# Down stage of a hybrid diffusion layer: earlier modulation rows, earlier first-half outputs, a longer last batch and another order of closing the tiles

## Chip, cores and metric

The kernel runs on one core of a Trainium2 chip. The metric is the device time of one execution in microseconds (us); lower is better. TensorE (PE) does the matmuls, VectorE (DVE), ScalarE (ACT) and GpSimd (POOL) the elementwise work, and SyncE (SP) issues most DMAs. Each engine works through its own queue in order, and semaphores order the engines among each other.

## What is computed

One layer of a diffusion backbone on 512 sample tokens and 128 prompt tokens with 1024 features: gated token mixers, then a feed-forward part with a short convolution. Only the last matrix product and what follows it are touched by the change:

```python
sh1, sc1, g1, sh2, sc2, g2 = jnp.split(mod, 6, axis=-1)   # mod = silu(c) @ w_ada + b_ada
...
h = rmsnorm(x, lw['norm2_g']) * (1.0 + sc2) + sh2
x = x + g2 * conv_ffn(h, ...)          # ends in (silu(g) * a) @ w_down, w_down is 2816 x 1024
...
y = rmsnorm(x, final_norm_g)           # x * rsqrt(mean(x*x) + EPS) * final_norm_g
```

So each output row needs both column halves of the down product before its mean square is known, and only then can it be scaled and stored.

## The kernel before

**Precision.** Each f32 operand is split into a high part (ScalarE, a copy that rounds to the matmul's type) and a low part (VectorE, the difference). A product is three matmuls: high with high, high with low, low with high.

**Blocks.** The 512 sample tokens are two blocks of 256, that is token tiles 0 and 1, and tiles 2 and 3; the 128 prompt tokens are tile 4. The 2816 inner features are two groups of 11 steps of 128 (called k steps), the 1024 output columns are two halves of 512. The sample part is a product of 2x2 blocks done in seven block products instead of eight (Winograd's form of Strassen's method). The prompt tile rides along in four of them.

**Units.** `PHASES` lists the seven products in the order 1, 5, 6, 2, 7, 4, 3; each is cut into six units of two k steps (the sixth has one), so there are 42 units, numbered u = 0 to 41 (`DOWN[u]` is phase and place j in it). A unit has a load (`down_load`), a preparation (`down_prep`: the splits, L1855 to L1859, after a sum of operands in `x_sum`) and its matmuls (`down_tile`, L1960). When unit i's matmuls are written, the load of unit i+5 and the preparation of unit i+3 have just been written (`ahead`). Five slots are cycled: a preparation overwrites what unit u-5 used. The fifth slot's weights lie in region X0 up to u = 28 and in A behind that.

**Units that are held back.** A unit in `JOIN` is kept and its matmuls are run together with the next ones, tile by tile, so that a tile is closed earlier than the others. Before, units (6,3) and (6,4) are held, and the last batch is (6,3), (6,4), (6,5): five k steps for tile 0, then five for tile 1, then for the prompt tile 4, which is cut into two column parts of 256 (`halved`), each with a PSUM bank of its own. What the prompt tile has gathered up to (6,2) is corrected and added to x by three VectorE instructions (L1967, then L1977 and L1981).

**What follows a product** is written in `down_start` and `down_out`. `LATER` names the phase and unit at which an output is written: `out_11(t)` forms the first column half of tiles 0, 1 and 4, `out_22(t)` the second half of tiles 2 and 3. Each is `joined`: a sum or difference with a kept product, the multiplication with the modulation row g2 (`gained`, L1977), the addition to the residual x (`added`, L1981), and a square with a row sum on ScalarE (`half_one`, L1986). The remaining halves come straight from the last products through `half_two`: `gained`, `added`, square with sum (L2045), joining both halves' sums (`half_join`, L2062), the root as a power of -0.5 on POOL (`down_root`, L2065), then scaling the one half on ScalarE (`down_scale`, L2073) and the other on VectorE (`down_gain`, L2080), and the store. `down_scale` expects its half to be multiplied with the final norm's gain already: that is `final_gain` on POOL (L2007).

**Modulation rows.** The last columns of w_ada (numbers 45, 46 and 47, which belong to g2) are made by VectorE in `col_make`: each is two multiplications with row sum over 128x1024 (L285). They are loaded by `col_load`. `gain_rows(1)` transposes the result on TensorE (L304), ScalarE copies it, SP writes it to DRAM (L308), and `gain_load` broadcasts it into S0 (L312). `COLS` and `G2` give the units at which this is done.

**Order.** The framework's scheduler may issue an instruction earlier than it is written, if it is ready. `tc.keep_in_program_order` (`keep_`) pins an instruction behind everything that was written before it for the same engine. `x2r` loads the residual tiles: 0 and 1 into X0, 2 and 3 into X1, 4 into G; these DMAs are pinned on SP.

Of the kernel before, what the change touches and what calls it, by code (L numbers as in the profile page):

```python
# [16 lines left out]
P = 128  # L17
# [53 lines left out]
def tile_step(ctx: ExitStack, tc: tile.TileContext, a: dict, outs: list, dbg=None):  # L71
# [54 lines left out]
    def nm(s):  # L126
        cnt[0] += 1
        return f"{s}_{cnt[0]}"

    def region(tag, shape, dt=F32):  # L130
        return big.tile(shape, dt, tag=tag, name=nm(tag))

    def pm():
        return psm.tile([P, 512], F32, tag="m", name=nm("m"))
# [165 lines left out]

    def gain_rows(i):

        m = pm() if i == 0 else acc["p"]
        ten.transpose(m[0:16, 0:P], gcol[:, i].rearrange("p v f -> p (v f)"), ident)  # L304
        pe(0.11)
        g = sp.tile([16, P], F32, tag="gr", name=nm("gr"), bufs=1)
        act(g, m[0:16, 0:P], AF.Copy)
        nc.sync.dma_start(growd[i], g)  # L308
# [1457 lines left out]
    def x2r(tag):  # L1766
        if tag not in x2v:
            r = x2v[tag] = region(tag, [P, 1280 if tag == "G" else 2560])
            for i in range(1 if tag == "G" else 2):
                sync(r[:, i * D:(i + 1) * D], x2d[i + dict(X0=0, X1=2, G=4)[tag]])  # L1770
        return x2v[tag]
# [36 lines left out]
    PHASES = [(1, "w", 0, (0, 0), 0), (5, "s", 0, (0, 1), 0), (6, "s", 1, (0, 0), None), (2, "w", 1, (1, 0), 1),  # L1808
              (7, "s", 2, (0, 1), None), (4, "s", 3, (1, 1), None), (3, "w", 3, (1, 0), 1)]
    DOWN = [(ph, j) for ph in range(7) for j in range(6)]  # L1810
    JOIN = {(4, 4), (5, 0), (6, 3), (6, 4)}

    def down_load(u):
        ph, j = DOWN[u]
# [24 lines left out]
    def down_prep(u, raw):  # L1839
        ph, j = DOWN[u]  # L1840
        ks, (p_, _, _, (h, c), hp) = KS[j], PHASES[ph]
        n = len(ks)
        if u % 5 < 3:
            w = wp.tile([P, 2, 2, 512], F32R, tag="w", name=nm("w"))
        elif u % 5 == 3:
            if "w4" not in fx:
                fx["w4"] = region("MG1", [P, 2, 2, 512], F32R)
            w = fx["w4"]
        else:
            w = region("X0" if u < 29 else "A", [P, 2, 2, 512], F32R)  # L1850
        if "xs" not in fx:
            fx["xs"] = region("XH", [P, 5, 2, 2, 256], F32R), region("MG0", [P, 5, 2, 2, P], F32R)
        s = [x[:, u % 5] for x in fx["xs"]]
        x_sum(p_, ks)
        act(w[:, 0, 0:n], raw, AF.Copy)  # L1855
        for x, r in zip(s, [x_raw(h, c, ks)] + ([xr["p", hp][:, ks[0]:ks[-1] + 1]] if hp is not None else [])):
            act(x[:, 0, 0:n], r, AF.Copy)
            vec.tensor_tensor(x[:, 1, 0:n], r, x[:, 0, 0:n].bitcast(F32), ALU.subtract)  # L1858
        vec.tensor_tensor(w[:, 1, 0:n], raw, w[:, 0, 0:n].bitcast(F32), ALU.subtract)  # L1859
        return w, s  # L1860
# [38 lines left out]
            pass  # L1899
        gain_col(f, ar[0])  # L1900

    COLS = dict(zip((23, 21, 19), range(47, 44, -1)))
    G2 = 27

    def down_start(u):
        ph, j = DOWN[u]
        if u == 0:
            acc["b1"], acc["b2"] = [pm(), pm()], [pm(), pm()]
            g0, g1 = pg(), pg()
            acc["p"], acc["q"], acc["b3"] = g0[:, 0, :], g0[:, 1, :], [g1[:, 0, :], g1[:, 1, :]]  # L1910
            r = region("XL1", [P, 5, 512])
            acc["c1"], acc["u2"], acc["cp"] = [r[:, 0], r[:, 1]], [r[:, 2], r[:, 3]], r[:, 4]
        for tag, part in {0: (("A", 0), ("B", 0)), 2: (("A", 1), ("B", 1)), 9: (("D", 0),), 11: (("D", 1),),
                          13: (("F", None),)}.get(u, ()):
            x_load(tag, part)
        if u == 5:
            x_tail(1, 1)
        if u == 16:
            x2[2:4] = [x2r("X1")[:, 0:1024], x2r("X1")[:, 1024:2048]]
        if u + 2 in COLS and COLS[u + 2] > 45:  # L1920
            col_load(COLS[u + 2])
        if u in COLS:
            col_make(COLS[u])
        if u == G2 - 1:
            gain_rows(1)
        if u == G2:
            grows["g2"] = gain_load(1, "S0")
            x2[4] = x2r("G")[:, 0:1024]
            r = region("H", [P, 2, 512])
            acc["u3"] = [r[:, 0], r[:, 1]]  # L1930
        if u == 28:
            x2[0:2] = [x2r("X0")[:, 0:1024], x2r("X0")[:, 1024:2048]]
        for f in LATER.get((ph, j), ()):
            f()

# [5 lines left out]
    def down_tile(u, ws):  # L1941
        ph, j = DOWN[u]
        p_, _, _, _, hp = PHASES[ph]
        down_start(u)
        hold.append((KS[j], ws))
        if (ph, j) in JOIN:
            return
        batch = hold[:]
        hold.clear()
        end = j == 5  # L1950
        for t in (0, 1, 4) if hp is not None else (0, 1):
            halved = p_ == 3 and t == 4 and end
            for ci, (c0, c1) in enumerate(((0, 256), (256, 512)) if halved else ((0, 512),)):
                ps = (acc["b1"][ci] if halved else bank(p_, t))[:, 0:c1 - c0]
                o = 0 if t == 4 else t * P
                for bi, (ks, (w, s)) in enumerate(batch):
                    for k in range(len(ks)):
                        for i, (hx, hw) in enumerate(((0, 0), (0, 1), (1, 0))):
                            first = ks[k] == 0 and i == 0 and (p_ in (1, 5) or p_ == 2 and t < 4) or halved and bi == k == i == 0
                            mm(ps, s[t // 4][:, hx, k, o:o + P], w[:, hw, k, c0:c1], start=first,  # L1960
                               stop=i == 2 and bi == len(batch) - 1 and k == len(ks) - 1, skip_group_check=True)
                        tick(0.65 * (c1 - c0) / 512)
                if end:
                    down_out(p_, t, c0, c1, ps)
        if p_ == 3 and j == 2:
            y = gp.tile([P, 512], F32, tag="gt", name=nm("y"))
            vec.tensor_tensor(y, acc["q"], acc["cp"], ALU.subtract)  # L1967
            gained(1, 4, 0, 512, y)
            added(1, 4, 0, 512)
# [19 lines left out]
    def down_out(p_, t, c0, c1, ps):  # L1989
        if p_ == 2 and t == 4:  # L1990
            act(acc["yp"], ps, AF.Copy)
        elif p_ in (1, 6):
            act(acc["cp"] if t == 4 else acc["c1" if p_ == 1 else "u2"][t], ps, AF.Copy)
        elif p_ == 7:
            act(acc["u3"][t], ps, AF.Copy)
        elif p_ == 4:
            half_two(0, t + 2, 0, 512, ps)
        elif p_ == 3:
            if t < 4:
                y = gp.tile([P, 512], F32, tag="gt", name=nm("y"))  # L2000
                keep_(vec.tensor_tensor(y, ps, acc["u2"][t], ALU.subtract))  # L2001
                ps = y
            half_two(1, t, c0, c1, ps)

    def final_gain(nh, t):
        xs = x2[t][:, nh * 512:nh * 512 + 512]
        pool.tensor_tensor(xs, xs, xr["F"][:, nh * 512:nh * 512 + 512], ALU.mult)  # L2007

    def final_gains():
        for nh, t in ((1, 2), (1, 3), (0, 0), (0, 1), (0, 4)):  # L2010
            final_gain(nh, t)
            if t in (2, 3):
                down_store(0, t)

    def joined(nh, t, ps, x, op):
        y = gp.tile([P, 512], F32, tag="gt", name=nm("y"))
        vec.tensor_tensor(y, ps, x, op)  # L2017
        gained(nh, t, 0, 512, y)
        added(nh, t, 0, 512)
        half_one(nh, t)  # L2020

    def out_11(t):
        if t == 4:
# [6 lines left out]
    def out_22(t):  # L2030
        joined(1, t + 2, acc["b2"][t], acc["u3"][t], ALU.subtract)

    LATER = {(5, 1): (lambda: out_22(0),), (5, 3): (lambda: out_22(1),), (5, 5): (lambda: out_11(0),),
             (6, 1): (lambda: out_11(1),), (6, 2): (lambda: out_11(4),), (6, 3): (final_gains,)}

    def half_two(nh, t, c0, c1, ps):
        xs = x2[t][:, nh * 512 + c0:nh * 512 + c1]
        q1, q2 = (st3[:, i + t:i + t + 1] for i in (8, 16))
        keep_(gained(nh, t, c0, c1, ps))
        if t == 4 and c0 == 0:  # L2040
            half_join(1, 8)
            down_root(1)
        keep_(added(nh, t, c0, c1))
        if c0 == 0:
            keep_(act(prods[t], xs, AF.Square, accum_out=q1))  # L2045
        if t == 1:
            down_store(nh, 0)
        elif t < 4:
            half_join(t, 8)
            down_root(t)  # L2050
        elif c0 > 0:
            half_join(t, 8)
            down_scale(nh, 1)
            keep_(vec.scalar_tensor_tensor(prods[t], xs, 1.0, xs, ALU.mult, ALU.mult, accum_out=q2))
            half_join(t, 16)
            down_root(t)
            down_gain(nh, 1)
            down_store(nh, t)

    def half_join(t, i):  # L2060
        q = st3[:, t:t + 1]
# [366 lines left out]
```

## Time and profile before

| what | us |
|---|---|
| median of three runs | 1009.75 (1008.81 to 1010.03) |
| profiled execution, its own time | 1008.12 |
| its span in the trace | 1006.0 |
| first matmul of the down stage | 858.4 |
| last matmul's end | 997.6 |

The span runs from the first to the last instruction. In a timeline a line gives the start, the length, the engine, the kernel's line, the operation and how many instructions were merged; matmuls are pipelined, so the spacing of their starts, not their length, is what one costs. TensorE's granted clock is full (1.00) in every stretch of the down stage up to 997.6.

### The profile page before, as it was taken

To read this page: it belongs to the slowest core of one execution; us is meant where nothing else is said; L and a number is where in the kernel's file an instruction comes from. 1 tells how busy PE (TensorE), PEld (TensorE's weight loads), DVE (VectorE), ACT (ScalarE), POOL (GpSimd) and SP (SyncE) were. 2 spreads that over 40 slices of the span, in tenths; PEclk is the share of its full clock that TensorE was granted. 3 is DMA by queue.
4 is the path that set the end of the run, shared out by engine and by line. 5 is a ranking of instruction groups with operands and counts; after the bars stand their busy time and mean duration, and the time that the engine had idled before them with its cause. 6 is when DMAs were issued, how large, how long until landed. Compare 5 with 4: busy or idle time off the path is not lost. (4 is left out here: it accounts for less than half of the span.)

```text
span 1006.0 us, 18962 instructions
## 1 busy us (share of the span) xinstructions
PE 993.2 (99%) x7503; PEld 941.0 (94%) x7503; DVE 825.0 (82%) x1381; ACT 558.5 (56%) x983; POOL 168.4 (17%) x223
## 2 busy tenths in 40 slices
PE   8999999999999999999999999999999999999996
PEld 7899999999999999999998899999999999888885
DVE  6678899867765767767768878999999998988897
ACT  6642343445554444445445476777777777656563
POOL 1000020323210221331010021222222222100023
PEclk9999999999999999999999999999999999999998
DMA  9875344496495498898258683866666666886462
GB/s 354 332 251 165 108 149 126 126 262 211 106 296 186 173 244 189 262 296 180 81 201 324 272 315 118 253 153 173 177 166 166 176 171 193 320 298 229 156 245 105
DMA packets 70009, 208.93 MB, mean 208 GB/s; under 512 B 9632, under 2 KB 24768, under 8 KB 67232
## 3 DMA queue, kind: packets, MB, share of 16 engines
q1 hardware_dynamic: 43536, 148.60, 41.8%
q0 software_dynamic: 26384, 59.12, 25.4%
q8 instruction: 59, 0.97, 0.4%
q14 instruction: 30, 0.25, 0.1%
HBM read 165.99 MB, written 48.51 MB: 213 GB/s over the span
## 5 line engine op out<-in xcount | busy, mean ns | idle before, releaser
L375 PE MATMUL g<-XH,w 128*128 128x320 f32 x704 | 171.2, 317 | 0.1
L375 PEld LDWEIGHTS g<-XH,w 128*128 128x128 f32 x704 | 120.6, 188 | 2.7 <-issue 1.0
L375 PE MATMUL g<-XL,w 128*128 128x320 f32 x352 | 108.7, 309 | 0.0
L375 PEld LDWEIGHTS g<-XL,w 128*128 128x128 f32 x352 | 66.3, 188 | 0.0
L1960 PE MATMUL m<-w,XH 128*128 128x512 f32 x246 | 58.6, 390 | 0.0
L1960 PEld LDWEIGHTS m<-w,XH 128*128 128x128 f32 x246 | 46.1, 188 | 9.7
L1152 PE MATMUL m<-XH,w 128*128 128x320 f32 x224 | 52.5, 309 | 0.0
L151 POOL DMA_DIRECT2D wsum<-in_w_dn_dram x36 | 36.5, 1158 | 53.1 <-issue 41.8
L151 DVE SCALAR_TENSOR_TENSOR X<-MG,p2t,X 128x641 f32<-128x641 f32 x44 | 38.9, 884 | 1.0 <-ACT X L151 0.2
L151 DVE SCALAR_TENSOR_TENSOR X<-X,p2t,X 128x641 f32<-128x641 f32 x44 | 38.9, 883 | 0.9
L151 ACT ACTIVATE w<-raw 128x1024 fp32r<-128x1024 f32 (+3 forms) x46 | 38.2, 851 | 2.1 <-DMA raw<-in_w_in_dram 1.1
L1512 PE MATMUL g<-XL,w 128*128 128x320 f32 x240 | 38.6, 310 | 0.0
L1152 PEld LDWEIGHTS m<-XH,w 128*128 128x128 f32 x224 | 38.3, 188 | 0.0
L1512 PE MATMUL g<-XL,C 128*128 128x320 f32 x240 | 38.3, 309 | 0.0
L1512 PEld LDWEIGHTS g<-XL,w 128*128 128x128 f32 x240 | 36.0, 188 | 0.6 <-ACT MG L151 0.3
L1512 PEld LDWEIGHTS g<-XL,C 128*128 128x128 f32 x240 | 36.0, 188 | 0.0
L1152 PE MATMUL m<-XL,w 128*128 128x320 f32 x112 | 34.6, 309 | 0.0
L151 ACT ACTIVATE ga<-m,cst 128x320 f32<-128x320 f32 x27 | 14.2, 528 | 36.6 <-PE m L1152 36.6
L1859 DVE TENSOR_TENSOR w<-raw,w 128x1024 fp32r<-128x1024 f32 (+1 forms) x26 | 30.1, 1159 | 3.3 <-ACT w L1855 3.3
L151 DVE TENSOR_TENSOR w<-raw,w 128x1024 fp32r<-128x1024 f32 (+2 forms) x36 | 30.6, 871 | 1.2 <-ACT w L151 1.2
L151 DVE TENSOR_TENSOR gb<-g,gb 128x640 f32<-128x640 f32 x12 | 9.9, 825 | 26.3 <-PE g L1165 25.4
L336 ACT ACTIVATE w<-raw 128x1024 fp32r<-128x1024 f32 (+1 forms) x22 | 24.3, 1104 | 12.2 <-PE m L947 8.2
(582 smaller groups left out, 2920.0 us busy)
## 6 DMA issues: line engine op xcount, KB each, us to landing
wsum<-in_w_dn_dram POOLq DMA_DIRECT2D x30, 512.0 KB, 12.1
raw<-in_w_up_dram SPq DMA_DIRECT2D x30, 512.0 KB, 5.3
raw<-in_w_gp_dram SPq DMA_DIRECT2D x21, 640.0 KB, 6.5
raw<-in_w_in_dram SPq DMA_DIRECT2D x19, 512.0 KB, 4.4
H<-in_w_adt_dram SPq DMA_DIRECT2D x19, 512.0 KB, 4.1
raw<-wsum SPq DMA_DIRECT2D x12, 512.0 KB, 4.4
actx<-X POOLq DMA_DIRECT2D x22, 256.0 KB, 5.0
wsum<-wsum POOLq DMA_DIRECT2D x10, 512.0 KB, 11.0
```

The source lines that it names most:

```text
L151: r = f(*args, **kw)
L336: high = lambda: act(w[:, 0], raw, AF.Copy)
L375: mm(o, w[:, h, k0 + k, :], r(k)[:, s], start=(k == 0 and i == 0), stop=(k == kt - 1 and i == 2))
L1152: mm(o, w[:, k, :], x[:, k, :], start=(first and k == 0 and j == 0), stop=(k == 3 and j == 2), skip_group_check=True)
L1512: z = mm(o, w[:, k, :], x[:, k, :], start=(first and k == 0 and j == 0), stop=(k == 3 and j == 2), skip_group_check=True)
L1859: vec.tensor_tensor(w[:, 1, 0:n], raw, w[:, 0, 0:n].bitcast(F32), ALU.subtract)
L1960: mm(ps, s[t // 4][:, hx, k, o:o + P], w[:, hw, k, c0:c1], start=first, stop=i == 2 and bi == len(batch) - 1 and k == len(ks) - 1, skip_gr ...
```

## The change

The last three modulation columns are made at units 9, 11 and 13 instead of 19, 21 and 23, and g2 is loaded at unit 16 instead of 27. The transposition uses another PSUM bank. The fifth weight slot lies in X1 (but for unit 4), so that X0 can take the residual of tiles 0 and 1 at unit 18, and X1 that of tiles 2 and 3 at unit 27. The first-half outputs `out_11(0)`, `out_11(1)`, `out_11(4)` are written at the first three units of the fifth phase (4,0) to (4,2) instead of (5,5), (6,1) and (6,2). The subtraction of a kept product from the last product's tiles 0 and 1 is taken out of the end: a new `out_less` multiplies the kept product with g2 and subtracts it from x at (4,3) and (4,4). The last batch has seven k steps ((6,2) is held too), and the prompt tile is cut into 320 and 192 columns. POOL's five final gains are pinned, written at (6,2) and (6,3), and the stores of tiles 2 and 3 behind the first two. In `half_two`, tile 0 is finished and stored at once, and tile 1 is joined, rooted, scaled and stored as soon as the first part of the prompt tile is added.

```diff
-        m = pm() if i == 0 else acc["p"]
+        m = pm() if i == 0 else acc["b3"][0]
...
-    JOIN = {(4, 4), (5, 0), (6, 3), (6, 4)}
+    JOIN = {(4, 4), (5, 0), (6, 2), (6, 3), (6, 4)}
...
-            w = region("X0" if u < 29 else "A", [P, 2, 2, 512], F32R)
+            w = region("X0" if u == 4 else "X1" if u < 29 else "A", [P, 2, 2, 512], F32R)
...
-    COLS = dict(zip((23, 21, 19), range(47, 44, -1)))
-    G2 = 27
+    COLS = dict(zip((13, 11, 9), range(47, 44, -1)))
+    G2 = 16
...
-        if u == 16:
-            x2[2:4] = [x2r("X1")[:, 0:1024], x2r("X1")[:, 1024:2048]]
+        if u == 18:
+            x2[0:2] = [x2r("X0")[:, 0:1024], x2r("X0")[:, 1024:2048]]
...
-        if u == 28:
-            x2[0:2] = [x2r("X0")[:, 0:1024], x2r("X0")[:, 1024:2048]]
+        if u == 27:
+            x2[2:4] = [x2r("X1")[:, 0:1024], x2r("X1")[:, 1024:2048]]
...
-            for ci, (c0, c1) in enumerate(((0, 256), (256, 512)) if halved else ((0, 512),)):
+            for ci, (c0, c1) in enumerate(((0, 320), (320, 512)) if halved else ((0, 512),)):
...
-        if p_ == 3 and j == 2:
+        if p_ == 3 and j == 1:
...
-            if t < 4:
-                y = gp.tile([P, 512], F32, tag="gt", name=nm("y"))
-                keep_(vec.tensor_tensor(y, ps, acc["u2"][t], ALU.subtract))
-                ps = y
             half_two(1, t, c0, c1, ps)
...
-        pool.tensor_tensor(xs, xs, xr["F"][:, nh * 512:nh * 512 + 512], ALU.mult)
-
-    def final_gains():
-        for nh, t in ((1, 2), (1, 3), (0, 0), (0, 1), (0, 4)):
+        keep_(pool.tensor_tensor(xs, xs, xr["F"][:, nh * 512:nh * 512 + 512], ALU.mult))
+
+    def final_gains(*which):
+        for nh, t in which:
             final_gain(nh, t)
-            if t in (2, 3):
-                down_store(0, t)
+
+    def stores():
+        for t in (2, 3):
+            down_store(0, t)
...
+    def out_less(t):
+        gained(1, t, 0, 512, acc["u2"][t])
+        xs = x2[t][:, 512:1024]
+        vec.tensor_tensor(xs, xs, prods[t], ALU.subtract)
...
-    LATER = {(5, 1): (lambda: out_22(0),), (5, 3): (lambda: out_22(1),), (5, 5): (lambda: out_11(0),),
-             (6, 1): (lambda: out_11(1),), (6, 2): (lambda: out_11(4),), (6, 3): (final_gains,)}
+    LATER = {(4, 0): (lambda: out_11(0),), (4, 1): (lambda: out_11(1),), (4, 2): (lambda: out_11(4),),
+             (4, 3): (lambda: out_less(0),), (4, 4): (lambda: out_less(1),), (5, 1): (lambda: out_22(0),), (5, 3): (lambda: out_22(1),),
+             (6, 2): (lambda: final_gains((1, 2), (1, 3)), stores),
+             (6, 3): (lambda: final_gains((0, 0), (0, 1), (0, 4)),)}
...
         keep_(gained(nh, t, c0, c1, ps))
+        keep_(added(nh, t, c0, c1))
+        if c0 == 0:
+            keep_(act(prods[t], xs, AF.Square, accum_out=q1))
         if t == 4 and c0 == 0:
             half_join(1, 8)
             down_root(1)
-        keep_(added(nh, t, c0, c1))
-        if c0 == 0:
-            keep_(act(prods[t], xs, AF.Square, accum_out=q1))
-        if t == 1:
-            down_store(nh, 0)
-        elif t < 4:
+            down_store(nh, 1)
+        elif t != 1:
             half_join(t, 8)
+            if t == 4:
+                keep_(vec.scalar_tensor_tensor(prods[t], xs, 1.0, xs, ALU.mult, ALU.mult, accum_out=q2))
+                half_join(t, 16)
             down_root(t)
-        elif c0 > 0:
-            half_join(t, 8)
-            down_scale(nh, 1)
-            keep_(vec.scalar_tensor_tensor(prods[t], xs, 1.0, xs, ALU.mult, ALU.mult, accum_out=q2))
-            half_join(t, 16)
-            down_root(t)
-            down_gain(nh, 1)
-            down_store(nh, t)
+            if t != 2 and t != 3:
+                down_store(nh, t)
```

## The prediction

> **What bounds the kernel now.** I read the page's busy shares and slices first, then a table of stretches of the down stage.
>
> ```profile
> span 1006.0 us, 18962 instructions
> PE 993.2 (99%) x7503; PEld 941.0 (94%) x7503; DVE 825.0 (82%) x1381; ACT 558.5 (56%) x983; POOL 168.4 (17%) x223
> ...
> 884.60:907.10 22.50, 22.50 (x101) 18.62 (x100) 18.39 (x30) 12.68 (x22) 0.00 (x0) 1.00 0.82 280
> 907.10:922.00 14.90, 14.90 (x67) 12.35 (x66) 12.99 (x18) 9.24 (x15) 0.00 (x0) 1.00 0.73 247
> ...
> 944.50:959.60 15.10, 15.10 (x69) 12.38 (x68) 10.94 (x14) 8.80 (x15) 0.00 (x0) 1.00 0.50 186
> 959.60:974.80 15.20, 15.20 (x67) 12.29 (x66) 15.17 (x21) 10.94 (x20) 5.03 (x3) 1.00 0.71 255
> ...
> 997.60:1006.00 8.40, 0.02 (x1) 0.00 (x0) 4.24 (x12) 3.18 (x7) 1.72 (x2) 0.66 0.48 187
> ```
>
> Columns are the stretch, its length, then PE, PEld, DVE, ACT and POOL busy, the clock, DMA share and GB/s. PE is busy in all of each stretch to 997.6; then comes a tail of 8.4 us without matmuls. The change leaves the number of products as it is, so it can win only in that tail or where PE's starts are spaced wider than a matmul needs. DVE has 4.16 us idle in the fifth phase (944.5 to 959.6) and none in the sixth (15.17 of 15.20). The timeline of PE shows what that costs, and what a matmul needs:
>
> ```profile
> 846.12 1.92 PE L1512 MATMUL g<-XH,w 128*128 128x320 f32 x12
> 847.88 1.92 PE L1512 MATMUL m<-XH,w 128*128 128x320 f32 x12
> ...
> 970.46 3.17 PE L1960 MATMUL m<-A,XH 128*128 128x512 f32 x12
> 973.47 4.24 PE L1960 MATMUL m<-w,XH 128*128 128x512 f32 x18
> ...
> 982.99 2.88 PE L1960 MATMUL m<-MG,XH 128*128 128x512 f32 x12
> ...
> 993.87 0.88 PE L1960 MATMUL m<-A,MG 128*128 128x256 f32 x6
> 994.58 1.24 PE L1960 MATMUL m<-w,MG 128*128 128x256 f32 x9
> 995.66 0.88 PE L1960 MATMUL m<-A,MG 128*128 128x256 f32 x6
> 996.38 1.24 PE L1960 MATMUL m<-w,MG 128*128 128x256 f32 x9
> ```
>
> From 982.99 (the start of unit (6,2)) to 993.87 there are 48 matmuls of 512 columns (18 of that unit, 15 each for tiles 0 and 1): 10.88/48 = 0.2267 us each. Unit 34 at 970.46 takes 3.01 us where 12 x 0.2267 = 2.72: 0.29 us of stall. This is the only stall of that size, so all stalls together are worth some tenths.
>
> **The tail, step by step.** The timeline of the end:
>
> ```profile
> 995.44 0.68 DVE L2001 TENSOR_TENSOR y<-m,XL 128x512 f32<-128x512 f32 x1
> ...
> 997.50 0.74 DVE L2080 SCALAR_TENSOR_TENSOR X<-X,st,F 128x512 f32<-128x512 f32 x1
> ...
> 998.16 0.42 DVE L1977 TENSOR_TENSOR dt<-m,S 128x256 f32<-128x256 f32 x1
> ...
> 998.72 0.72 POOL L2065 TENSOR_TENSOR st<-st,neghalf 128x1 f32<-128x1 f32 x1 [2.57 <-DVE st L2062]
> 998.95 0.42 DVE L1977 TENSOR_TENSOR dt<-m,S 128x256 f32<-128x256 f32 x1
> ...
> 999.40 0.42 DVE L1981 TENSOR_TENSOR G<-G,dt 128x256 f32<-128x256 f32 x1
> ...
> 999.75 0.15 DVE L2062 SCALAR_TENSOR_TENSOR st<-st 128x1 f32<-128x1 f32 x1
> 999.86 0.42 DVE L2054 SCALAR_TENSOR_TENSOR dt<-G 128x256 f32<-128x256 f32 x1
> ...
> 1000.33 0.16 DVE L2062 SCALAR_TENSOR_TENSOR st<-st 128x1 f32<-128x1 f32 x1
> ...
> 1000.57 0.99 POOL L2065 TENSOR_TENSOR st<-st,neghalf 128x1 f32<-128x1 f32 x1 [1.12 <-DVE st L2062]
> 1001.59 0.72 ACT L2073 ACTIVATE G<-G,st 128x512 f32<-128x512 f32 x1 [1.40 <-POOL st L2065]
> ...
> 1002.41 0.33 SPq L1761 DMA_DIRECT2D out_dram<-G  x1
> ```
>
> PE's last matmul (996.38 + 1.24) ends at 997.62, but VectorE takes up the prompt tile's last part only at 998.95, 1.33 us later: it is still closing tile 1 (from 995.44). From 998.95 on nothing else is in the way, and it takes 7.04 us to the end at 1005.99 (3.58 of it behind the store's issue). That queue is what the change attacks.
>
> **PE's end after the change.** The last batch has 21 matmuls for tile 0 and 21 for tile 1, 42 x 0.2267 = 9.52 us, then 21 of 320 columns at (847.88 - 846.12)/12 = 0.1467, 3.08 us, then 21 of 192. That width isn't in the trace. The 256-column ones cost (995.66 - 993.87)/15 = 0.119; the nearest narrower ones are 128 columns wide:
>
> ```profile
> 572.07 1.03 PE L1339 MATMUL m<-cst,C 128*128 128x128 f32 x8
> 572.86 0.95 PE L1295 MATMUL m<-w,B 128*128 128x512 f32 x3
> ```
>
> 8 in 0.79 us, 0.099. Half the width saves only 0.02, so I take 0.11 for 192: 2.31 us (2.08 to 2.50). Sum 14.91 us against 10.88 + 30 x 0.119 = 14.45 before: PE ends **0.46 us later** (0.23 to 0.65). The Trainium skill, "TensorE: Matmul & The Clock Gate", section "LDWEIGHTS (loading the stationary operand)", gives a weight load as columns / 1.2 ns: 107 ns for 128 columns, whatever the matmul's width. An estimate from that page is 2.24 us for the 21, and PE's end 0.39 us later; the row of 0.099 lies below that figure.
>
> **VectorE's chain in the new tail.** Tile 1 needs no subtraction now (0.68 us, L2001, gone), and nothing of it is left when the prompt tile comes. The 320 part's last matmul starts and drains by 982.99 + 9.52 + 3.08 + 0.16 = 995.75 (0.16 is 1.92 - 1.76 of the rows at 846 and 847). `gained` for 320 columns: 256 take 0.42 and 512 take 0.68, so 64 columns are 0.065. The starts then follow with the old spacings (0.45 to `added`, 0.35 to the join, 0.24 to POOL), the first two 0.065 longer: 995.80, 996.32, 996.74, POOL at 996.98. POOL's root took 0.72 and 0.99 above; I take 0.72, so tile 1's `down_gain` starts at 997.73 and frees VectorE 0.67 later, at 998.40 (998.67 with 0.99; 998.23 with 0.55, the least of the five roots). PE's last part ends at 995.59 + 2.31 + 0.16 = 998.06, so it is VectorE behind POOL that decides, and PE's lost 0.46 us is hidden behind it. The last part is now 192 wide: three instructions shorter by 0.065 each, 7.04 - 0.20 = 6.84 us from its start. End: 998.40 + 6.84 = **1005.24, 0.75 us before 1005.99**. The bounds are -0.92 and -0.48.
>
> **What is moved, and its cover.**
> - The three columns: 6 multiplications of 1.22 us plus sums, some 2.8 us each, 8.4 in all, leave units 19 to 23 and fall into units 9 to 13, behind which TensorE waits in order for the transposition at unit 15.
>
> ```profile
> L285 DVE SCALAR_TENSOR_TENSOR H<-H,S 128x1024 f32<-128x1024 f32 x2 | 2.4, 1218 | 0.0
> ...
> 909.00 1.22 DVE L1859 TENSOR_TENSOR w<-raw,w 128x1024 fp32r<-128x1024 f32 x1
> ...
> 915.22 6.96 PE L1960 MATMUL m<-w,XH 128*128 128x512 f32 x30
> ```
>
>   From 884.6 to 922 VectorE is idle 4.11 + 1.91 = 6.0 us. Unit 16's preparation ends at 910.22 and its matmuls come at 915.22 + 2.72 = 917.94: 7.7 us ahead. With two columns (5.6) before it and some 4 us of idle used it is done by about 912, and the third column by 914.7, half a microsecond before unit 15. I cost it at nothing; without that cover it is 0 to 1.5 us. SP's wait for the copy of the transposed rows moves with it, with unit 21's load queued behind; that unit's matmuls start four units later or more, so it is covered.
> - The first-half outputs: three VectorE instructions of 0.68 for each of tiles 0 and 1 with a 0.15 sum (2.2 each), two for tile 4 (1.5), and `out_less` 2 x 1.36: 8.6 us, into a stretch with 4.16 idle. Out of the stretch 944.5 to 974.8 go `out_11(0)` (2.2) and POOL's three gains, which lengthen VectorE's work beside them:
>
> ```profile
> 962.44 2.03 POOL L2007 TENSOR_TENSOR X<-X,F 128x512 f32<-128x512 f32 x1 [87.26 <-DMA X<-x2d]
> 963.30 1.71 DVE L1977 TENSOR_TENSOR dt<-y,S 128x512 f32<-128x512 f32 x1
> ...
> 970.71 1.78 DVE L1859 TENSOR_TENSOR w<-raw,w 128x512 fp32r<-128x512 f32 x1
> ...
> 984.79 2.33 POOL L2065 TENSOR_TENSOR st<-st,neghalf 128x1 f32<-128x1 f32 x1 [2.25 <-DVE st L2062]
> 987.10 1.50 POOL L2007 TENSOR_TENSOR X<-X,F 128x512 f32<-128x512 f32 x1
> 988.56 1.30 POOL L2007 TENSOR_TENSOR G<-G,F 128x512 f32<-128x512 f32 x1
> ```
>
>   1.71 instead of 0.68 is 1.03 a time, 3.1 for three. Net 8.6 - 2.2 - 3.1 = +3.3 us against 4.16 idle; and `out_less` (2.7) has its inputs early and can fill the hole that the columns leave. So no new stall, and I leave unit 34's 0.29 as it is.
> - POOL's five gains, pinned now, run behind tile 3's root (984.79 before). The Trainium skill, "GPSIMD Engine Reference", section "8. Key points", says that GpSimd shares its SBUF interfaces with VectorE and contends with instructions of two SBUF inputs; the trace agrees (1.71 against 0.68). The rule speaks against putting five of them in the last batch.
>
> **The rivals.**
> 1. *VectorE runs late in the fifth and sixth phases* (slower). Its idle time there is waiting for slots that PE frees, so it may not be usable; then the 3.3 us arrive at unit 34, which already stalls, and PE ends 3.3 later: 1009.0 + 3.3 = 1012.3. The kernel is slower than before once less than 2.5 us of the idle is usable (3.3 - 0.75), and by over 0.2% when almost none is, or when the transposition waits as well. For it: 15.17 busy of 15.20, so nothing gives way there. Against it: the columns' 8.4 us are gone ahead of it. Chance 0.30, 0.24 of it beyond 0.2%.
> 2. *POOL's queue holds tile 0.* Five gains of 1.3 to 2.0, 7.8 us, end at 991.8 if tile 3's root is done at 984 and at 994.9 if at 987.1 as before. Tile 0's root waits behind them, and VectorE waits pinned at tile 0's `down_gain`. It decides from 993.0 on: then tile 1's join comes after 996.74, and each us is lost. At worst +1.9: 1010.9. Chance 0.15.
> 3. *The best case*: the stall of unit 34 goes, and both last roots take 0.55 (0.17 and 0.44 less): -0.75 - 0.29 - 0.61 = -1.65: 1008.1, and with luck in the measurement (1008.81 to 1010.03 in three runs) beyond 2 us. Chance 0.10.
>
> **How the numbers follow.** Forecast, chance 0.45: 1005.24 in the span, 1007.4 for the profiled execution (2.1 us lie around the span), and 1009.75 - 0.75 = **1009.0** against the median of the runs. Its own range is 1008.2 (stall gone as well, -1.2, and the measurement) to 1009.8. The range for 8 in 10 reaches down to rival 3 less the runs' spread, 1007.6, and up past most of rival 1, 1012.8. Faster by over 0.2% (2.0 us, about what a measurement can tell) needs more than the sum holds: 0.10. Slower by over 0.2% is the larger part of rival 1: 0.24. The rest, with the forecast, rival 2 and a short stall of rival 1: 0.66.
>
> **What would show it.** Right: the last L1977 on VectorE at 192 columns starts at about 998.4, less than 0.5 us behind PE's end, and L2001 is gone; PE's spacing in units 24 to 38 stays 0.2267. Wrong: a PE gap of over 1 us at units 15 or 30 to 38 (rival 1), or tile 0's L2065 starting after 993 behind five L2007 (rival 2).

## The result and the profile after

| | before | changed |
|---|---|---|
| median of 13 runs each, us | 1009.15 (1008.34 to 1010.22) | 1007.01 (1006.37 to 1008.11) |
| ratio, 95% interval | | 0.9978 (0.9970 to 0.9987) |
| profiled execution, its own time, us | 1008.12 | 1007.80 |
| its span, us | 1006.0 | 1006.0 |

The change makes the kernel 2.1 us faster (1.3 to 3.0). A second series on another occasion gave 1006.93 against 1008.82, ratio 0.9982 (0.9973 to 0.9991). The two profiled executions have the same span, so the first thing to learn from them is why. The timeline of TensorE for the changed kernel, in the second, third and sixth phase and in the last batch:

```profile
884.67 2.88 PE L1960 MATMUL m<-w,XH 128*128 128x512 f32 x12
888.38 1.65 PE L1960 MATMUL g<-w,MG 128*128 128x512 f32 x6 [0.83 <-ACT XL L1993]
...
913.67 2.88 PE L1960 MATMUL m<-X,XH 128*128 128x512 f32 x12
916.82 0.27 PE L304 MATMUL g<-cst,gcol 128*16 128x128 f32 x1 [0.27 <-DVE gcol L291]
916.84 3.45 PE L1960 MATMUL m<-w,XH 128*128 128x512 f32 x14
...
972.03 2.88 PE L1960 MATMUL m<-A,XH 128*128 128x512 f32 x12
974.75 4.24 PE L1960 MATMUL m<-w,XH 128*128 128x512 f32 x18
...
984.27 1.52 PE L1960 MATMUL m<-MG,XH 128*128 128x512 f32 x6
...
993.79 1.04 PE L1960 MATMUL m<-MG,MG 128*128 128x320 f32 x6
...
996.87 0.81 PE L1960 MATMUL m<-MG,MG 128*128 128x192 f32 x6
...
998.19 1.17 PE L1960 MATMUL m<-w,MG 128*128 128x192 f32 x9
```

Twelve matmuls from 884.67 should last 2.72 us; the next row starts 3.71 later. This stall in unit 6, about 1.1 us with what follows it, belongs to single executions. The chain of waits of this trace has the transfer before it in one row:

```profile
870.51 12.35 DMA B<-actx
```

It is a load of activations for the second phase. That this load makes the stall is not shown: in another trace with a stall of 1.06 us (`G2 = 18` below) the chain has a different load before it, of 10.15 us. The stall is there with 0.35 us or more in 8 of the 16 traces of this study, with either closing, and smaller or missing in the others, among them the one of before. And TensorE waits in order at 916.82 for the third modulation column: 913.67 + 2.72 = 916.39, so 0.45 us are lost.

So single times mislead here, and I compare the traces from a fixed point: the start of the matmuls of unit (6,2), 982.99 before and 984.27 after. "Batch" is from there to the end of the last matmul, "tail" from there to the end of the span. Before: 14.63 + 8.37 = 23.00. After: 998.19 + 1.17 = 999.36, so 15.08 + 6.60 = **21.68**. The tail on the other engines:

```profile
994.00 0.69 DVE L1977 TENSOR_TENSOR dt<-m,S 128x512 f32<-128x512 f32 x1
...
997.07 0.49 DVE L1977 TENSOR_TENSOR dt<-m,S 128x320 f32<-128x320 f32 x1 [1.66 <-PE m L1960]
...
998.24 0.55 POOL L2066 TENSOR_TENSOR st<-st,neghalf 128x1 f32<-128x1 f32 x1 [5.08 <-DVE st L2063]
...
999.49 0.35 DVE L1977 TENSOR_TENSOR dt<-m,S 128x192 f32<-128x192 f32 x1
...
1000.90 0.55 POOL L2066 TENSOR_TENSOR st<-st,neghalf 128x1 f32<-128x1 f32 x1 [2.12 <-DVE st L2063]
...
1002.30 0.33 SPq L1761 DMA_DIRECT2D out_dram<-G  x1
```

VectorE now waits for TensorE (1.66 us at 997.07) where before it ran behind it, and takes the last part up 0.13 us after TensorE's end instead of 1.33. What follows takes 6.5 us instead of 7.0: the last root, on POOL, takes 0.55 us instead of 0.99. The fifth and sixth phase in the stretches shown of before:

```profile
944.50:959.60 15.10, 15.10 (x69) 12.49 (x68) 14.50 (x24) 11.42 (x21) 0.00 (x0) 1.00 0.60 216
959.60:974.80 15.20, 15.20 (x69) 12.59 (x68) 15.20 (x25) 11.09 (x19) 0.00 (x0) 1.00 0.61 191
```

VectorE's 10.94 us of the fifth phase have become 14.50, and in this trace that stretch begins 1.7 us ahead of the phase: from 946.19 to 961.15, the fifth phase itself, VectorE is busy in all of the 14.96 us. POOL has nothing to do in the sixth, and TensorE starts unit 34 (at 972.03) to 35 (974.75) 2.72 us apart: the stall of 0.29 us is gone.

### The profile page after: what moved, and what is told of

It reads as the page before. It is cut to its first block, busy times and chain, and to the rows that moved or that the text cites. A ratio compares the mean times of both kernels' runs of the same rounds, so it can differ in the third digit from the quotient of the medians.

```text
span 1006.0 us, 18975 instructions
## 1 busy us (share of the span) xinstructions
PE 993.6 (99%) x7509; PEld 941.4 (94%) x7509; DVE 825.5 (82%) x1383; ACT 559.1 (56%) x983; POOL 166.4 (17%) x223
## 4 chain that ended last, share of the span: by engine, by line
PE 86%; DVE 5%; DMA 4%; issue 2%; ACT 2%; POOL 1%; SPq 0%; POOLq 0%; DVEq 0%; ACTq 0%
PE g L1512 20%; PE m L1152 17%; PE g L375 14%; PE m L1960 6%; PE g L1165 5%; PE m L1512 4%; PE m L1295 3%; PE g L1960 3%; PE g L947 2%; PE g L1295 2%; PE m L151 2%; PE g L151 1%; DMA B<-actx 1%; PE m L539 1%; PE m L1507 1%
```

## The experiments

Each kernel's trace was read like the two above. Medians stand beside those of the kernel before on the same chip. "Stalls" are TensorE's in units 14 to 15 and 26 to 34, without the random ones ahead of them.

| kernel | median, us | before, us | ratio (95%) | stalls | batch | tail | batch + tail |
|---|---|---|---|---|---|---|---|
| before | | | | 0.42 | 14.63 | 8.37 | 23.00 |
| changed | 1007.01 | 1009.15 | 0.9978 (0.9970-0.9987) | 0.56 | 15.08 | 6.60 | 21.68 |
| changed, again | 1006.93 | 1008.82 | 0.9982 (0.9973-0.9991) | 0.13 | 15.08 | 6.59 | 21.67 |
| before, new closing | 1012.18 | 1008.82 | 1.0032 (1.0020-1.0045) | 0.43 | 15.08 | 10.74 | 25.82 |
| before, gains pinned | 1008.91 | 1008.67 | 1.0001 (0.9992-1.0010) | 0.13 | 14.63 | 9.07 | 23.70 |
| before, rows moved | 1009.46 | 1008.85 | 1.0007 (0.9998-1.0015) | 1.02 | 14.63 | 9.23 | 23.86 |
| before, rows and slots moved | 1009.36 | 1008.75 | 1.0005 (0.9996-1.0015) | 0.13 | 14.63 | 9.24 | 23.87 |
| changed, old closing | 1007.62 | 1008.82 | 0.9986 (0.9977-0.9995) | 0.53 | 14.63 | 7.09 | 21.72 |
| changed, subtraction at the end | 1006.79 | 1008.67 | 0.9984 (0.9975-0.9993) | 0.13 | 15.08 | 6.61 | 21.69 |
| changed, old closing, subtraction at the end | 1007.21 | 1008.67 | 0.9984 (0.9975-0.9993) | 0.13 | 14.63 | 7.09 | 21.72 |
| ... and outputs 1 and 4 late | 1007.65 | 1008.85 | 0.9986 (0.9978-0.9995) | 0.53 | 14.63 | 7.64 | 22.27 |
| ... and all three outputs late | 1008.31 | 1008.75 | 0.9997 (0.9988-1.0006) | 0.13 | 14.63 | 8.55 | 23.18 |
| changed, gains free | 1006.61 | 1008.67 | 0.9983 (0.9974-0.9992) | 0.30 | 15.08 | 6.59 | 21.67 |
| changed, five k steps | 1007.01 | 1008.85 | 0.9980 (0.9971-0.9989) | 0.13 | 14.89 | 7.27 | 22.16 |
| changed, row two units later | 1006.62 | 1008.82 | 0.9977 (0.9969-0.9986) | 0.11 | 15.08 | 6.61 | 21.69 |
| ... and 256 + 256 columns | 1006.63 | 1008.85 | 0.9975 (0.9965-0.9984) | 0.11 | 14.71 | 6.70 | 21.41 |

**The changed kernel again** (no edit).

> The changed kernel once more, for a second trace. Theory (the tail is 1.7 us shorter and the last batch 0.45 us longer, so 1.3 us come from the closing; the rest from TensorE's stalls, which differ from run to run): 2.1 us faster than before, give or take 0.5; the stall of 1.1 us at the first units of the second phase need not be there again, the 0.56 us around unit 15 is. Rival (the tail is all, and the two medians differed by chance): 1.3 us faster.

1.9 us faster, as expected. Unit 6 didn't stall this time (unit 0 did, by 0.48 us), nor, against the expectation, did TensorE wait ahead of unit 15 beyond the transposition's own 0.13. Batch and tail repeat to 0.01 us, which is what makes them worth comparing.

**The new closing alone.** In the kernel before, `half_two`, `JOIN`, the column parts and the correction are taken from the changed one.

```diff
-    JOIN = {(4, 4), (5, 0), (6, 3), (6, 4)}
+    JOIN = {(4, 4), (5, 0), (6, 2), (6, 3), (6, 4)}
-            ... ((0, 256), (256, 512)) if halved ...
+            ... ((0, 320), (320, 512)) if halved ...
-        if p_ == 3 and j == 2:
+        if p_ == 3 and j == 1:
...
```

> The kernel before with the new closing alone: the new half_two, 320 and 192 columns, seven k steps, the correction one unit earlier. The rows, the first-half outputs, the subtraction and the free gains stay as before. Theory (closing and missing subtraction work together: with the subtraction VectorE has 1.4 us more between tile 0 and the prompt tile, and the first-half outputs of tiles 1 and 4 fall into the last batch): half of the gain or less, 0 to 0.8 us faster than before. Rival (the order of closing alone carries it): 1.3 us faster.

Both missed: it is 3.4 us slower than before. VectorE's timeline:

```profile
992.29 2.48 DVE L2076 SCALAR_TENSOR_TENSOR X<-X,st,F 128x512 f32<-128x512 f32 x2
994.69 0.68 DVE L2001 TENSOR_TENSOR y<-m,XL 128x512 f32<-128x512 f32 x1
...
997.61 0.16 DVE L2058 SCALAR_TENSOR_TENSOR st<-st 128x1 f32<-128x1 f32 x1 [0.79 <-ACT dt L2042]
998.43 0.75 DVE L2076 SCALAR_TENSOR_TENSOR X<-X,st,F 128x512 f32<-128x512 f32 x1 [0.67 <-POOL st L2061]
999.10 0.68 DVE L2001 TENSOR_TENSOR y<-m,XL 128x512 f32<-128x512 f32 x1
```

Tile 0's product is taken up at 994.69, because the first-half outputs and the scaling of tiles 2 and 3 are in the queue. The new closing then makes VectorE wait twice (0.79 for the square, 0.67 for POOL's root) before it touches tile 1 at 999.10, 0.2 us before TensorE is done with everything. Behind a queue that is late the new closing costs time.

**The old closing in the changed kernel** (the same edit backwards).

> The changed kernel with the old closing: the old half_two, the prompt tile in 256 and 256 columns, a last batch of five k steps. The moved outputs, the moved rows and the pinned gains stay. Theory (the closing is worth 1.7 - 0.45 = 1.3 us): 1.0 to 1.3 us slower than the changed kernel, less what the missing subtraction saves there; TensorE ends 0.45 us earlier, the tail is back to about 8 us. Rival (what wins is the missing subtraction and the earlier outputs, not the order of closing): within 0.4 us of the changed kernel.

The rival was right: TensorE ends 0.45 us earlier, the tail is 0.49 longer, together 21.72 against 21.68. The medians differ by 0.7 us, but their intervals overlap, the lowest times (1006.21 here, 1006.38 for the changed kernel) don't differ that way, and this kernel's profiled execution shows 0.88 us in unit 6. So it is the traces that speak for the rival; the medians leave it open.

**The subtraction back at the end, with either closing.**

```diff
-             (4, 3): (lambda: out_less(0),), (4, 4): (lambda: out_less(1),), (5, 1): ...
+             (5, 1): ...
         elif p_ == 3:
+            if t < 4:
+                y = gp.tile([P, 512], F32, tag="gt", name=nm("y"))
+                keep_(vec.tensor_tensor(y, ps, acc["u2"][t], ALU.subtract))
+                ps = y
```

> The changed kernel with the subtraction back at the end (tiles 0 and 1, L2001's work of 0.72 us each) and without out_less; everything else as changed. Theory (VectorE sets the closing, and a subtraction of tile 1 stands in its chain): tile 1 is added 0.7 us later, still before the prompt tile's first part at 997, so the tail grows by 0 to 0.3 us only. Rival (the subtraction carries the gain): 0.7 to 1.4 us slower than the changed kernel.

> The changed kernel with the old closing and with the subtraction at the end: what is left is the moved rows, the moved first-half outputs and the pinned gains. Theory (the shorter tail under the old closing, 7.09 against 8.37 us, comes from the subtraction's two times 0.7 us): tail back to 8.2 to 8.5 us, 1.2 us slower than with the old closing alone. Rival (it comes from the outputs that no longer stand in the last batch): tail stays at 7.1 to 7.4 us.

Taking the subtraction out is worth nothing: 21.69 and 21.72 with it, 21.68 and 21.72 without. Under the new closing the tail is 0.01 us longer, the lower end of the theory's 0 to 0.3; under the old one the rival was right. With the old closing and the subtraction, VectorE takes up tile 1 here:

```profile
994.15 0.69 DVE L2001 TENSOR_TENSOR y<-m,XL 128x512 f32<-128x512 f32 x1 [0.25 <-PE m L1960]
```

It waits for TensorE there; before it was 995.44 and no wait. What is left in this kernel is the rows, the first-half outputs and POOL's gains.

**The first-half outputs put back**, in that kernel, first those of tiles 1 and 4, then all.

```diff
-    LATER = {(4, 0): (lambda: out_11(0),), (4, 1): (lambda: out_11(1),), (4, 2): (lambda: out_11(4),),
+    LATER = {(4, 0): (lambda: out_11(0),),                      # second kernel: (5, 5)
...
+             (6, 1): (lambda: out_11(1),), (6, 2): (lambda: out_11(4), ...),
```

> The kernel with the old closing and the subtraction at the end (tail 7.09 us), but the first-half outputs of tiles 1 and 4 back at (6,1) and (6,2), where the kernel before had them; out_11(0), the rows and the pinned gains as changed. Theory (these outputs stand in VectorE's queue ahead of the last products and make tiles 0 and 1 late by 1.4 to 1.8 us): tail 8.2 to 9.1 us, 1.2 us or more slower than without this edit. Rival (it is out_11(0) and the fifth phase that count): tail stays at 7.1 to 7.4 us.

> Old closing, subtraction at the end, and all three first-half outputs where the kernel before had them, (5,5), (6,1) and (6,2); rows, slots and pinned gains as changed. Theory (the outputs carry the gain, all three of them): batch and tail together 22.7 us or more against 21.72 with all three early and 22.27 with out_11(0) early; unit 34 does not stall, as POOL's gains are pinned. Rival (out_11(0) does not matter, the pinned gains and the order of the stores do): 22.2 to 22.4 us.

The tail goes from 7.09 to 7.64 with two of them late, less than the theory had, and to 8.55 with all three. So all three count: 0.55 us for tiles 1 and 4, 0.91 for tile 0 (with the other two late already; the other order was not run), 1.46 together, and the time is back at that of before (1008.31 against 1008.75). VectorE's rows with all three late:

```profile
985.32 1.66 DVE L1981 TENSOR_TENSOR G<-G,dt 128x512 f32<-128x512 f32 x1
987.84 0.15 DVE L1987 TENSOR_SCALAR st<-st 128x1 f32<-128x1 f32 x1 [0.85 <-ACT dt L1986]
...
995.80 0.69 DVE L2001 TENSOR_TENSOR y<-m,XL 128x512 f32<-128x512 f32 x1
```

The output of tile 4 is still being added at 985, behind the start of unit (6,2) at 983.17, its square costs a wait of 0.85, and tile 1 is taken up at 995.80 without any wait for TensorE.

**The rows alone, and the rows with the slots.** In the kernel before, `COLS`, `G2` and the PSUM bank are changed; in the second kernel also the fifth slot and the residual's loads are.

```diff
-    COLS = dict(zip((23, 21, 19), range(47, 44, -1)))
-    G2 = 27
+    COLS = dict(zip((13, 11, 9), range(47, 44, -1)))
+    G2 = 16
```

> The kernel before with the modulation rows alone moved (columns at units 9, 11 and 13, the load at 16, the other PSUM bank). Theory (the rows only make room; the gain is in the outputs that may then be written earlier): tail 8.2 to 8.5 us, unit 34 stalls by 0.3 us as before, same time as before within 0.4 us. Rival (8.4 us less of VectorE's work behind unit 18 already frees the closing): 0.8 us or more faster than before, tail near 7.1 us.

> The kernel before with the rows, the weight slot in X1 and the loads of the residual moved; no output, gain or closing moved. Theory (rows and slots only make room): same time as before within 0.6 us, batch and tail together 23 to 24 us; the time around the span is 1.8 us, as in the other kernels with moved rows, if the rows or loads are what shortens it, and 2.1 us if the outputs are. Rival (the residual of tiles 0 and 1 in time for POOL's gains lets them run early): 1 us faster than before.

Neither gains anything; batch and tail are 0.9 us longer than in the kernel before, more than expected of the first. In the second kernel tile 0 is taken up 10.24 us after the start of unit (6,2) instead of 9.39, and this row has most of it:

```profile
987.41 1.67 DVE L1981 TENSOR_TENSOR G<-G,dt 128x512 f32<-128x512 f32 x1
```

The addition for tile 4 takes 1.67 us instead of 0.69 (at 986.75 before), and one of POOL's free gains now runs beside it, from 986.86 to 988.52. With rows alone the wait around unit 14 was 0.89 + 0.13 us. Unit 34 didn't stall in either, against the expectation. They only make room.

**POOL's gains, pinned in the kernel before and free in the changed one.**

```diff
-        pool.tensor_tensor(xs, xs, xr["F"][:, nh * 512:nh * 512 + 512], ALU.mult)
+        keep_(pool.tensor_tensor(xs, xs, xr["F"][:, nh * 512:nh * 512 + 512], ALU.mult))
```

> The kernel before with POOL's five final gains pinned where they are written, at (6,3), and nothing else. Theory (three gains at 962 to 972 lengthen VectorE's work beside them by 1.03 us each and so make unit 34's stall): the stall of 0.29 us at unit 34 is gone; but the gains now run one after the other at 987 to 995, beside VectorE's closing, and hold back tile 0's root there: tail the same or up to 1 us longer. Rival (unit 34 is late because of the first-half output written at (5,5), not because of POOL): the stall stays.

> The changed kernel with POOL's five gains free again. Theory (contention in the sixth phase makes stalls): the gains move up into the fifth and sixth phases and a stall of 0.3 us or more comes back between units 28 and 36; the closing is 0 to 0.4 us shorter because POOL is free for the roots. Rival: no stall, since VectorE has room there now; same time or 0.2 us faster.

Pinned in the kernel before, unit 34 takes its 2.72 us, so its stall hung on where POOL's gains run:

```profile
970.92 2.88 PE L1960 MATMUL m<-A,XH 128*128 128x512 f32 x12
973.64 3.56 PE L1960 MATMUL m<-w,XH 128*128 128x512 f32 x15
```

But the gains then run at 984.7 to 992.1 and the tail is 0.7 us longer: by the trace 0.4 us lost, too little for the ratio (1.0001) to show. Free in the changed kernel, no stall came back: there the rival was right, and pinning is worth nothing. It isn't always so: the kernel with rows and slots moved (23.87) and the one with all three outputs late (23.18) differ only in the gains, which the second has pinned and in part written one unit earlier, and in the order of two stores, and 0.69 us lie between them.

**Five k steps in the last batch** of the changed kernel.

```diff
-    JOIN = {(4, 4), (5, 0), (6, 2), (6, 3), (6, 4)}
+    JOIN = {(4, 4), (5, 0), (6, 3), (6, 4)}
-        if p_ == 3 and j == 1:
+        if p_ == 3 and j == 2:
```

> The changed kernel with a last batch of five k steps ((6,2) runs by itself, the correction one unit later); 320 and 192 columns and the new closing stay. Theory (the second prompt part must be long enough to cover tile 1's chain of 2.4 us; with 15 matmuls of 0.11 it lasts 1.65): TensorE ends 0.3 us earlier, but the last part waits about 0.8 us for VectorE; 0.2 to 0.6 us slower than the changed kernel. Rival (tile 1 is long done): 0.3 us faster.

As the theory had it: TensorE ends at 997.91, but VectorE takes the last part up at 998.71, and batch and tail are 0.48 us longer. The median (1007.01) can't show that.

**Two better values.** The transposition two units later (`G2 = 18`), and then the prompt tile in halves as well.

```diff
-    G2 = 16
+    G2 = 18
-            ... ((0, 320), (320, 512)) if halved ...
+            ... ((0, 256), (256, 512)) if halved ...
```

> The changed kernel with the transposition of the modulation row at unit 17 instead of 15 and its load at 18. Theory (TensorE waits in order at unit 15 for the third modulation column, 0.56 us in the trace): that stall goes, 0.4 to 0.6 us faster than the changed kernel. Rival (VectorE is late there anyway, and the wait reappears at units 16 to 18 for a preparation): no gain.

> The changed kernel with the transposition two units later and the prompt tile in 256 and 256 columns. Theory (a matmul of 192 columns costs 0.11 and one of 256 0.12 us, 320 costs 0.147: two of 256 are 0.018 us cheaper a pair, 0.36 us over 21; the last three VectorE instructions are 0.065 us longer each): batch 14.7 us, tail 6.8, 0.15 us faster than with the transposition alone moved. Rival (tile 1's chain is not covered by the shorter first part): VectorE takes the last part up 0.3 us or more behind TensorE and nothing is won.

The wait ahead of unit 15 is gone in both although unit 6 stalled by 1.07 and 0.82 us. Halves are 0.28 us shorter, by 0.37 in the batch for 0.09 in the tail. This last version has the lowest ratio to the kernel before, 0.9975; against the changed kernel the 0.28 us of the halves are shown by the traces, while the intervals overlap; the later transposition wins something only in executions in which unit 15 waits.

## Why the prediction was wrong

Forecast -0.75 us, measured -2.1 and -1.9; 1007.01 lies below the range, and the gain is larger than the best case of -1.65. Part of the distance from the forecast 1009.0 is its base: three runs of before had a median of 1009.75, thirteen had 1009.15.

The step of the sum that failed is the price of POOL's two last roots. The prediction carried them over from the old order of closing, 0.72 us for tile 1 and 0.99 (inside the 7.04) for the prompt tile. In the new order VectorE is idle beside both, and both took 0.55: 0.61 us less. With the old closing put back in the changed kernel they take 0.72 and 0.99 again. The prediction has the contention between POOL and VectorE, and applies it to the long gains only. Two terms left as they were add to it, unit 34's stall (0.29) and the time outside the span (0.33): -0.75 - 0.61 - 0.29 - 0.33 = -1.98.

A second step failed without moving the number. The sum starts from a VectorE that is free when the first part of the prompt tile ends ("nothing of it is left when the prompt tile comes"), and the only reason that it gives is the missing subtraction. The time was right: forecast 995.80, measured 997.07, which is 995.79 when the later start of the batch (984.27 against 982.99) is taken off. The reason was wrong: by the runs it is the moved first-half outputs that free VectorE, and these the prediction costed only in the fifth phase, where it asked for "no new stall". So the start of the chain came out by luck, while the signs that the prediction had named for being right were all there (the last part within 0.5 us of TensorE's end, no L2001, no stall in units 24 to 38). Its account from the traces:

- **TensorE's longer batch**: forecast +0.46, measured 15.08 - 14.63 = +0.45. A matmul of 192 columns is (998.19 - 996.87)/12 = 0.11, as taken.
- **The tail**: forecast 1.21 us shorter (0.75 + 0.46), measured 1.77. The last part is taken up 0.13 us behind TensorE, forecast 0.34. The roots' 0.17 and 0.44 us are the difference but for 0.05.
- **What makes batch and tail shorter**: one edit after the other, they go from 23.00 (before) to 23.87 with the rows and slots moved, 23.18 with the gains pinned, 22.27 with tile 0's output early, 21.72 with those of tiles 1 and 4, 21.72 without the subtraction and 21.68 with the new closing. The closing's own share is 0.49 us of tail for 0.45 of batch. The sizes hold in this order only: pinning costs 0.70 in the kernel before, and the new closing costs 2.82 there. The prediction took tile 1's own work (from 995.44) for the queue, but VectorE was late before that, at tile 0:

```profile
988.43 2.20 PE L1960 MATMUL m<-w,XH 128*128 128x512 f32 x9
...
992.38 0.68 DVE L2001 TENSOR_TENSOR y<-m,XL 128x512 f32<-128x512 f32 x1
```

  Tile 0's last matmul ends at 990.63, and VectorE takes the tile up 1.7 us later.
- **Stalls**: unit 34's 0.29 us were left in the forecast though the same paragraph removed their cause, POOL's gains; they went. The transposition's own 0.13 us moved from unit 26 to unit 15.
- **Outside the span**: in before, a run's time is 2.08 to 2.22 us longer than its span, in the changed kernel 1.77 to 1.88: 0.33 us in the mean that no row shows and that the prediction took as fixed. The two kernels with only rows, or rows and slots, moved and the one with all outputs late spread over both (1.72 to 2.14 run by run). Its cause stays open.

Sum: 21.68 - 23.00 = -1.32, stalls -0.29, outside -0.33: -1.94, against -1.9 and -2.1, if the random stalls of both kernels are alike.

Of the rivals, the first is refuted: VectorE's idle time of the fifth phase was usable, all of it, and TensorE didn't stall. Its side case, the wait for the third column at unit 15, came with about 0.4 us in three executions in which unit 6 had stalled (0.89 in the kernel with the rows alone), and with 0.18 in one that had stalled in unit 0, inside its 0 to 1.5; it did not come in the kernel with rows and slots, where unit 6 had stalled by 0.35. The second did not come: POOL's five gains ended at 990.97, and POOL then sat idle for 1.64 us until VectorE's join let tile 0's root start at 992.61, which is 991.3 on the prediction's time, before the 993.0 from which it would have decided. A wait of VectorE for a pinned root is seen with the new closing in the old kernel, 0.67 us at tile 0 and 0.66 at tile 1, a part of the 2.82 us that it costs there. The third came in full: the stall went and both roots took 0.55, -1.61 by the traces against its -1.65; the rest is outside the span.

## What to carry to other kernels

Work that is moved out of a closing stretch must be credited there, not only costed where it goes: an in-order queue that is 1.7 us late at the first of three closings is late at all of them. A price read from the old order, as the root's 0.99 us beside VectorE's scaling, is to be asked again for the new one. The new order of closing cost 2.82 us behind a late queue and won 0.04 behind a free one; test it alone before giving it the gain. When executions differ by a random stall of the same size as the effect, compare the traces from a fixed point behind it.

## What the runs showed of the hardware

A root of 128x1 on POOL took 0.55 us when VectorE was idle (the three at 992.61, 998.24 and 1000.90 of the changed kernel) and 0.99 when VectorE multiplied two SBUF operands beside it: with the old closing back in the changed kernel the last root is 0.99 again, here in the kernel that has the subtraction at the end too. In before, tile 0's root at 995.60 took 0.55 although VectorE was at work beside it (L2001, from 995.44), with one of its two operands in PSUM.

```profile
999.20 0.74 DVE L2089 SCALAR_TENSOR_TENSOR X<-X,st,F 128x512 f32<-128x512 f32 x1
...
999.36 0.99 POOL L2074 TENSOR_TENSOR st<-st,neghalf 128x1 f32<-128x1 f32 x1 [1.20 <-DVE st L2071]
```

So the contention that the prediction has for the long gains was seen with an instruction of one element per partition too; the new closing avoids it by scaling tile 1 before the last root.
